# One decoder layer on one core: the first conv products on rows not yet normed, and conv taps ahead of their count from the heads' queries on

## The chip, the cores and the metric

The kernel runs on one core of a Trainium2 chip. The metric is device microseconds of one execution, start to end. TensorE is PE in the profile (its weight loads are PEld), VectorE is DVE, ScalarE is ACT, GpSimd is POOL, and SyncE, which issues most transfers, is SP.

## The reference

One layer of a decoder over 256 rows of 1024 channels, in fp32. Cut to what the change touches:

```python
n = RMSNorm(x)                       # x * rsqrt(mean(x*x) + eps) * g
a, gate, q, k, v, qi, ki, wi, gc, ga = split(n @ w_in)
u = a * sigmoid(gate)
u = causal_depthwise_conv(u, conv_w)           # 31 taps on each of 1024 channels
u = silu(LayerNorm(u)) @ w_conv_out
attn = top-k attention of q, k, v (keys chosen by qi, ki, wi), 8 heads
h = x + (gate_c * u + gate_a * attn @ w_attn_out) @ w_mix_out
h = h + CrossAttn(RMSNorm(h), RMSNorm(mem))    # xq, xk, xv, 4 heads
h = h + W2 relu(W1 RMSNorm(h))**2
return RMSNorm(h)
```

## The kernel before

Activations lie feature-major: a tile holds 128 channels on the partitions and the 256 rows along them. The weights are streamed from HBM in chunks of 1 MB, in a fixed order, by SP. Each half chunk is split into two parts for a matmul in fp32r: `hi` is a rounded copy (ScalarE, line 315) and `lo` is raw − hi (VectorE). The activations are split in the same way (n_p, o_p and so on). A product is then two matmuls for each tile of 128 channels, a wide one of hi against both parts and a narrow one of lo against the high part.

The first chunk, ("conv", 0), is an exception. It isn't split: PE multiplies it in native fp32, by n_f, the normed rows in full precision. It holds two tiles of products, the gate (`ps_conv00`) and the value (`ps_conv01`), eight products each. Behind it PE goes on with wide matmuls on n_p.

The norm at the start goes like this. PE transposes x_rm (the rows) to pt_n, ScalarE and VectorE scale it by the gain g_first to xg, the squares of the rows are summed meanwhile, and GpSimd takes the power −0.5 of them to rs_n (`power`). PE spreads rs_n over the partitions with two transposes against the identity, to ps_rsb_n (`spread`). VectorE multiplies xg by it to n_f, and n_f is split into n_p.

The 31 taps of the causal convolution run on VectorE, as acc += u · cw; some are made by ScalarE as products and added by a DMA of GpSimd, and some go by fours (ring and four). They are put into the order by `tick()`, which the code calls between its products. It keeps two sums of model time, pe.total and dve.total, in ns, and issues taps while

```python
while (...) and dve.total < pe.total - 1000:
    fill_one()
...
dve.total = max(dve.total, pe.total - 2000)
```

holds. The engines take their instructions in the order in which the program issues them, so this count decides only where the taps stand in VectorE's order, not when they run. When the taps of all channels are in, the last sums (usum, the sum over the eight tiles of acc) are added by VectorE, and `layer_norm` begins at the next tick: PE multiplies usum by a matrix of 1/1024 to ps_mub (the mean), VectorE subtracts it from acc, ScalarE squares, PE sums the squares to ps_vr, and ps_rsb spreads the reciprocal root of that. The chain is a generator, and takes a step at each tick. The product "co" reads its result.

Each head of the attention is a generator too: scores ps_s from q and k, a softmax on VectorE and ScalarE (att_t, att_p, sm), transposes ps_pt, the product ps_o with v, and its split to o_p (ScalarE the high part, VectorE the low). Products stand between these steps: q and k of the heads, then xk and xv of the cross attention (in kv), then ao.

PSUM banks come in three tags: mm (2), acc (4) and aux (2). `ps_turn` alternates between mm and acc.

Of the kernel before, what the change touches and what calls it, by code (L numbers as in the profile page):

```python
# [8 lines left out]
F32 = mybir.dt.float32  # L9
F32R = mybir.dt.float32r  # L10
BF16 = mybir.dt.bfloat16
AF = mybir.ActivationFunctionType
ALU = mybir.AluOpType
# [3 lines left out]
P = 128  # L17
D = 1024
S = 256
KT = D // P  # L20
# [101 lines left out]
def block_kernel(ctx, tc, x, xt, mem, memt, wst, wki, vecs, convw, gout, out):  # L122
    nc = tc.nc
    ctx.enter_context(tc.manual_schedule())
    pe = Counted(nc.tensor, pe_price)
    dve = Counted(nc.vector, dve_price)
    act = nc.scalar.activation
# [10 lines left out]
    def t8(name, dt=F32, shape=(P, KT, S)):  # L138
        return big.tile(list(shape), dt, tag="t8", bufs=12, name=name)
# [4 lines left out]
    def w2(name, dt=F32, shape=(P, 512)):  # L144
        return work.tile(list(shape), dt, tag="w2", bufs=8, name=name)
# [4 lines left out]
    def bank(tag, bufs, name):  # L150
        return psum.tile([P, 512], F32, tag=tag, bufs=bufs, name=name)

    def ps_mm(name):
        return bank("mm", 2, name)
# [4 lines left out]
    def ps_aux(name):  # L159
        return bank("aux", 2, name)  # L160

    mm_turn = [0]

    def ps_turn(name):

# [4 lines left out]
    prepared, whole, elsewhere = {}, {}, set()  # L170
# [5 lines left out]
    def fetch(c, raw, parts=1, only=None):  # L176

        key = STREAM[c]
        n = KT * NK if key[0] == "ki" else N_CHUNK
        src = wki if key[0] == "ki" else wst[INDEX[key]]  # L180
        for q in range(parts):
            if only in (None, q):
                ns = slice(q * n // parts, (q + 1) * n // parts)
                nc.sync.dma_start(raw[:, ns], src[:, ns])
        raw_of[c] = raw
        landed.update((key, q) for q in ((0, 1) if only is None else (only,)))

    def load(parts=1):
        if not order:
            return  # L190
        c = order.pop(0)
        key = STREAM[c]
        fetch(c, t8(f"raw{c}", F32, (P, N_CHUNK)) if c in early else raws.tile([P, N_CHUNK], F32, tag="raw", name=f"raw{c}"),
              2 if key in BY_HALVES else parts)
        if key[0] == "f2" and key[1] in ADDED:
            t = sums_of[c] = t8(f"sums{c}", F32, (P, 4, 512))
            blocks = wst[INDEX[key]].rearrange("p (j n) -> p j n", j=4)
            nc.gpsimd.dma_start(t[:, 0:2, :], blocks[:, 0:4:3, :])
            if key[1] == ALL_ADDED:
                nc.gpsimd.dma_start(t[:, 2:4, :], blocks[:, 0:4:2, :])  # L200
            nc.gpsimd.dma_start(t[:, 0:2, :], blocks[:, 1:2, :].to_broadcast([P, 2, 512]), accum_op=ALU.add)
            if key[1] == ALL_ADDED:
                nc.gpsimd.dma_start(t[:, 2:4, :], t[:, 1:2, :].to_broadcast([P, 2, 512]), accum_op=ALU.add)
                nc.gpsimd.dma_start(t[:, 3, :], blocks[:, 0, :], accum_op=ALU.add)
        if key in WHOLE:
            whole[key] = raw_of[c].rearrange("p (k n) -> p k n", k=2 * KT)
        elif c < FIRST:
            high_jobs.extend(jobs_of(c))
        elif c == FIRST:
            high_jobs.extend(last_jobs())  # L210
# [10 lines left out]
    def jobs_of(c):  # L221
        key = STREAM[c]
        if key[0] == "f2" and key[1] in SEVEN:
            return seven(key, c)
        n = KT * NK if key[0] == "ki" else N_CHUNK
        parts = 1 if key[0] == "ki" else 2
        ns = [slice(q * n // parts, (q + 1) * n // parts) for q in range(parts)]
        return [Stage((*key, q), lambda q=q: high(key, c, ns[q], q, q == parts - 1), slot=key != ("f2", 15),
                      needs=(key, q)) for q in range(parts)]
# [94 lines left out]
    def split_high():  # L324
        if high_jobs and high_jobs[0].here() and (not high_jobs[0].slot or nsplit[0] - nused[0] < HALVES - held[0]):
            job = high_jobs.pop(0)
            nsplit[0] += job.slot
            while job.steps:
                job.step()
            job.high()  # L330

    def split_low():
        if low_jobs:
            low_jobs.pop(0)()
        for job in high_jobs[:3]:
            if job.steps and job.here():
                job.step()
                break

    nsplit, nused, held = [0], [0], [1]  # L340
# [11 lines left out]
    chains, fours, fill, turn, done, ended = [], [], [], [0], [], []  # L352
# [16 lines left out]
    def split_ahead():  # L369
        split_low()  # L370
        split_high()

    def tick():
        for c in list(chains):
            if next(c, "end") == "end":
                chains.remove(c)
        while (len(fill) > 1 or (fill and (len(ended) > 5 or nused[0] < 5))) and dve.total < pe.total - 1000:
            fill_one()
        if fours and next(fours[0], "end") == "end":
            fours.clear()  # L380
        dve.total = max(dve.total, pe.total - 2000)
        add_some()

    def fill_one():

        some = [q for q in fill[:3] if q is not turn[0]] or fill
        q = some[0] if len(some[0]) < 10 and len(fill) > 3 else max(some, key=len)
        turn[0] = q
        q.pop(0)()
        if not q:  # L390
            fill.remove(q)
# [9 lines left out]
    def split(hi, lo, src):  # L401
        act(hi, src, AF.Copy)
        dve.tensor_tensor(out=lo, in0=src, in1=hi.bitcast(F32), op=ALU.subtract)
# [116 lines left out]
    half = cst.tile([P, 2], F32, name="half")  # L520
# [10 lines left out]
    ps = ps_aux("ps_warm")  # L531
# [22 lines left out]
    def spread(cols, name):  # L554

        ps = ps_aux(f"ps_{name}")
        for rb in range(2):
            pe.transpose(ps[:, rb * P : rb * P + P], cols[:, rb : rb + 1].to_broadcast([P, P]), ident)
        return ps[:, :S]
# [3 lines left out]
    n_f = t8("n_f")  # L563
    ss = small.tile([P, 2], F32, tag="ss", name="ss_n")
    ptn = [ps_acc(f"pt_n{c}") for c in range(4)]
    xg = t8("xg")
# [4 lines left out]
    for rb in range(2):  # L571
        for kt in range(KT):
# [5 lines left out]
                             in1=x_rm[:, 1, D // 2 :], scale=1.0 / D, scalar=EPS, op0=ALU.mult, op1=ALU.add,  # L578
                             accum_out=ss2[:, 1:2])
    dve.tensor_tensor(out=ss, in0=ss, in1=ss2, op=ALU.add)  # L580
    rs_n = power(ss, "n")
    rsb_n = spread(rs_n, "rsb_n")
    for kt in range(KT):
        src = ptn[kt // 2][:, (kt % 2) * S : (kt % 2) * S + S]
        if kt in (4, 6):
            dve.tensor_scalar(xg[:, kt, :], src, g_first[:, kt : kt + 1], None, ALU.mult)
        else:
            act(xg[:, kt, :], src, AF.Copy, scale=g_first[:, kt : kt + 1])
    for lo, hi in ((0, 1), (1, 2), (2, 4), (4, 6), (6, 8)):
        dve.tensor_tensor(out=n_f[:, lo:hi, :], in0=xg[:, lo:hi, :],  # L590
                          in1=rsb_n.unsqueeze(1).to_broadcast([P, hi - lo, S]), op=ALU.mult)
    for c in range(0, KT, 2):
        split(n2.high(c, 2), n2.low(c, 2), n_f[:, c : c + 2, :])
    split_high()
    split_low()
    split_high()
    pe.total = dve.total = 0.0

# [31 lines left out]
    u = t8("u")  # L630
# [74 lines left out]
    def conv_tile(i, half):  # L705
        key = ("conv", i)
        w = weights("conv", i, half, KT) if key not in WHOLE else None
        split_ahead()
        ps = (ps_turn if i > 0 else ps_mm)(f"ps_conv{i}{half}")
        if w:  # L710
            tile_b(ps, w, n2, wide=i > 0, back=back[0])
            back[0] = i > 0 and not back[0]
        else:
            for kt in range(KT):
                pe.matmul(ps[:, :S], whole[key][:, half * KT + kt, :], n_f[:, kt, :], start=kt == 0, stop=kt == KT - 1)
        return ps

    def conv_in(i):
        psg = conv_tile(i, 0)
        sg = w2(f"sg{i}", F32, (P, S))  # L720
        if i > 0:
            merge_now(sg, psg)
            act(sg, sg, AF.Sigmoid)
        else:
            act(sg, psg[:, :S], AF.Sigmoid)
        tick()
        psa = conv_tile(i, 1)
        if i > 0:
            merge_now(u[:, i, :], psa)
        dve.tensor_tensor(out=u[:, i, :], in0=u[:, i, :] if i > 0 else psa[:, :S], in1=sg, op=ALU.mult)  # L730
        tick()
        tap(i, 0)()
        queue = [tap(i, s) for s in range(1, TAPS) if s not in (*delays.get(i // 2, ()), *by_four.get(i // 4, ()))]
        queue.append(last_tap(i))
        if i // 2 not in delays:
            fill.append(queue)
        else:
            queues.setdefault(i // 2, []).append(queue)
            if i % 2:
                delay = iter(delays[i // 2])  # L740
                ready[i // 2] = lambda: add_tap(i // 2, next(delay))
        if ("conv", i) in WHOLE:
            load()

    for i in range(4):
# [10 lines left out]
    ps = ps_mm("ps_ki")  # L756
# [191 lines left out]
        headed.append(h)  # L948

    heads, headed = [], []  # L950

    def qk(name):
        return big.tile([P, 2, S], F32, tag="qk", bufs=4, name=name)
# [661 lines left out]
```

## Time and profile before

| | |
|---|---|
| time, median of 3 runs | 497.76 us (497.68 to 498.03) |
| profiled execution | 497.77 us |
| its span | 495.8 us |
| mean granted clock of TensorE | 0.997 |
| ScalarE busy | 377.6 us (76%) |
| GpSimd busy | 50.5 us (10%) |
| DMA, mean over the span | 223 GB/s, 110.36 MB |

The span runs from the first to the last instruction of the core, and the time of the execution holds 1.97 us around it. A timeline row of the profile has the start in us, the us from the first start to the last end of its group, the engine, the line, the operation, out<-in, the shape, how many instructions (x) and in brackets the idle time before them and what ended it. L87 is the line of the counting helper, so most instructions of PE and DVE carry it, and the names tell them apart.

### The profile page before, as it was taken

The page shows a single profiled execution, that of the slowest core. Times are in us where ns is not written, and L with a number is a line of the kernel's source. Part 1 is how long each engine was busy: PE and PEld are TensorE (multiplying, and loading weights), DVE is VectorE, ACT ScalarE, POOL GpSimd, SP SyncE. Part 2 cuts the span into 40 slices and gives each one's busy share as a digit, 9 for nine tenths or more (in the row PEclk, how much of TensorE's full clock was granted, in tenths as well). Part 3 has the DMA queues.
Part 4 walks back from the last instruction along what each step waited for, and adds up shares of the span by engine and source line. Part 5 has one row for each costly group of instructions (what it writes and reads, how often), then busy time and mean ns, then how long its engine had stood idle before and what let it go on. Part 6 is the DMA issues. An engine that isn't in the chain of part 4 may idle for free.

```text
span 495.8 us, 7787 instructions
## 1 busy us (share of the span) xinstructions
PE 486.5 (98%) x2832; PEld 428.0 (86%) x2832; DVE 460.1 (93%) x826; ACT 377.6 (76%) x677; POOL 50.5 (10%) x67
## 2 busy tenths in 40 slices
PE   7999999999999999999999999999999999999995
PEld 5888888888888889888889999988998888888884
DVE  5899999999999979989988987899999999999986
ACT  7578879998977787757946658687777878878852
POOL 2002211222011211000000000000010101121000
PEclk9999999999999999999999999999999999999998
DMA  8948676989987977354645552766979868999802
GB/s 315 380 190 262 191 190 212 277 234 248 283 247 215 243 166 209 134 171 169 254 171 177 205 203 97 278 193 144 255 263 296 247 238 258 283 318 341 260 3 85
DMA packets 33430, 110.36 MB, mean 223 GB/s; under 512 B 11104, under 2 KB 13408, under 8 KB 24432
## 3 DMA queue, kind: packets, MB, share of 16 engines
q1 hardware_dynamic: 24416, 93.03, 53.7%
q0 software_dynamic: 8688, 16.64, 17.6%
q8 instruction: 22, 0.36, 0.3%
q10 hardware_dynamic: 288, 0.20, 0.1%
q14 instruction: 16, 0.13, 0.1%
HBM read 99.29 MB, written 1.05 MB: 202 GB/s over the span
## 4 chain that ended last, share of the span: by engine, by line
PE 96%; DVE 1%; DMA 1%; ACT 1%; issue 0%; SPq 0%; DVEq 0%
PE ps_f L87 18%; PE ps_p L87 15%; PE ps_conv L87 9%; PE ps_co L87 5%; PE ps_ao L87 5%; PE ps_mix L87 5%; PE ps_k L87 5%; PE ps_ga L87 4%; PE ps_gc L87 4%; PE ps_q L87 4%; PE ps_v L87 4%; PE ps_xo L87 3%; PE ps_xq L87 2%; PE ps_xk L87 2%; PE ps_qi L87 2%; PE ps_xv L87 2%
## 5 line engine op out<-in xcount | busy, mean ns | idle before, releaser
L87 DVE TENSOR_TENSOR lo<-raw,hi 128x1024 fp32r<-128x1024 f32 x133 | 161.4, 1216 | 2.0 <-ACT hi L315 1.8
L315 ACT ACTIVATE hi<-raw 128x1024 fp32r<-128x1024 f32 x133 | 138.7, 1048 | 5.0 <-DMA raw<-in_wst_dram 5.0
L87 PE MATMUL ps_f<-ff_p,hi 128*128 128x512 f32 (+1 forms) x320 | 72.3, 347 | 0.0
L87 PEld LDWEIGHTS ps_f<-ff_p,hi 128*128 128x128 f32 x320 | 56.3, 189 | 7.9
L87 DVE SCALAR_TENSOR_TENSOR acc<-u,cw,acc 128x241 f32<-128x241 f32 (+25 forms) x142 | 58.9, 467 | 0.2
L87 PE MATMUL ps_f<-ff_p,lo 128*128 128x256 f32 x256 | 46.9, 283 | 0.0
L87 PEld LDWEIGHTS ps_f<-ff_p,lo 128*128 128x128 f32 x256 | 39.3, 191 | 1.8
L703 POOL DMA_DIRECT2D acc<-products x25 | 21.7, 879 | 123.3 <-ACT products L702 43.7
L87 PE MATMUL ps_conv<-n_p,hi 128*128 128x512 f32 x112 | 29.1, 396 | 0.0
L87 PEld LDWEIGHTS ps_conv<-n_p,hi 128*128 128x128 f32 x112 | 20.3, 188 | 4.5 <-issue 0.7
L293 ACT ACTIVATE inner<-sums 128x1024 fp32r<-128x1024 f32 x13 | 13.8, 1059 | 10.9 <-DVE sums L87 10.9
L702 ACT ACTIVATE products<-u,cw 128x243 f32<-128x243 f32 (+19 forms) x50 | 22.1, 492 | 0.0
L87 DVE TENSOR_TENSOR ft<-ft 128x128 f32<-128x128 f32 (+2 forms) x49 | 19.7, 401 | 1.1 <-ACT ft L1327 0.6
L671 ACT ACTIVATE ring<-u,cw 128x236 f32<-128x236 f32 (+10 forms) x44 | 20.2, 480 | 0.0
L87 PE MATMUL ps_p<-outer,fs 128*128 128x512 f32 x78 | 20.2, 394 | 0.0
L87 PE MATMUL ps_v<-hi,n_p 128*128 128x512 f32 x64 | 19.9, 389 | 0.0
L87 PE MATMUL ps_p<-inner,fs 128*128 128x512 f32 x78 | 19.8, 390 | 0.0
L87 PE MATMUL ps_co<-u_p,hi 128*128 128x512 f32 (+1 forms) x80 | 19.3, 350 | 0.0
L87 PE MATMUL ps_mix<-mix_p,hi 128*128 128x512 f32 (+1 forms) x80 | 19.2, 349 | 0.0
L87 PE MATMUL ps_k<-n_p,hi 128*128 128x512 f32 x64 | 17.4, 404 | 0.0
L87 PE MATMUL ps_q<-n_p,hi 128*128 128x512 f32 x64 | 17.3, 402 | 0.0
L87 PEld LDWEIGHTS ps_p<-inner,fs 128*128 128x128 f32 x78 | 14.6, 188 | 3.0
(443 smaller groups left out, 1212.4 us busy)
## 6 DMA issues: line engine op xcount, KB each, us to landing
raw<-in_wst_dram SPq DMA_DIRECT2D x67, 1024.0 KB, 5.9
raw<-in_wst_dram SPq DMA_DIRECT2D x28, 512.0 KB, 5.8
sums<-in_wst_dram POOLq DMA_DIRECT2D x15, 512.0 KB, 7.6
acc<-products POOLq DMA_DIRECT2D x25, 256.0 KB, 6.1
x_rm<-in_x_dram SPq DMA_DIRECT2D x2, 512.0 KB, 4.0
mem_rm<-in_mem_dram SPq DMA_DIRECT2D x1, 1024.0 KB, 8.7
mem_t<-in_memt_dram SPq DMA_DIRECT2D x1, 1024.0 KB, 10.7
h_t<-in_xt_dram SPq DMA_DIRECT2D x1, 1024.0 KB, 7.7
```

The source lines that it names most:

```text
L87: return fn(*args, **kwargs)
L293: act(hi, src, AF.Copy)
L315: act(hi, raw[:, ns], AF.Copy)
L671: act(dst[:, t, :], u[:, 4 * g + t, : S - s], AF.Copy, scale=cw[:, 4 * g + t, TAPS - 1 - s : TAPS - s])
L702: act(prod[:, a, s:], u[:, t, : S - s], AF.Copy, scale=cw[:, t, TAPS - 1 - s : TAPS - s])
L703: nc.gpsimd.dma_start(acc[:, ts, :], prod, accum_op=ALU.add)
```

## The change

It has three parts.

1. The native products read xg, the rows with the gain but not yet divided by their root mean square. Two products of `ps_conv00` stand ahead of the transposes of rs_n in PE's order, the six others and those of `ps_conv01` behind them. The missing factor, one per row, is brought in later: ScalarE copies ps_rsb_n to SBUF (`rsb`) behind the second n_p, VectorE multiplies ps_conv00 by it ahead of the sigmoid, and multiplies the sigmoid's result by it ahead of the product with ps_conv01. One `split_low` moves from the start to behind `conv_in(0)`.
2. `mm_turn` begins at 1, so every bank that `ps_turn` gives changes its tag.
3. The count of the taps gets its 1000 from `spare[0]`, and that is −1500 from the heads' queries on: taps are issued until dve.total is 1500 ahead of pe.total, not until it is 1000 behind.

```diff
-    mm_turn = [0]
+    mm_turn = [1]
...
+    spare = [1000]
     def tick():
...
-        while (len(fill) > 1 or (fill and (len(ended) > 5 or nused[0] < 5))) and dve.total < pe.total - 1000:
+        while (len(fill) > 1 or (fill and (len(ended) > 5 or nused[0] < 5))) and dve.total < pe.total - spare[0]:
             fill_one()
...
-    rsb_n = spread(rs_n, "rsb_n")
...
+    first = whole["conv", 0]
+    ps_first = ps_mm("ps_conv00")
+    def first_products(kts):
+        for kt in kts:
+            pe.matmul(ps_first[:, :S], first[:, kt, :], xg[:, kt, :], start=kt == 0, stop=kt == KT - 1)
+    first_products(range(2))
+    rsb_n = spread(rs_n, "rsb_n")
+    rsb = w2("rsb", F32, (P, S))
...
         split(n2.high(c, 2), n2.low(c, 2), n_f[:, c : c + 2, :])
+        if c == 2:
+            act(rsb, rsb_n, AF.Copy)
     split_high()
-    split_low()
     split_high()
...
+        if (i, half) == (0, 0):
+            first_products(range(2, KT))
+            return ps_first
...
-                pe.matmul(ps[:, :S], whole[key][:, half * KT + kt, :], n_f[:, kt, :], start=kt == 0, stop=kt == KT - 1)
+                pe.matmul(ps[:, :S], whole[key][:, half * KT + kt, :], xg[:, kt, :], start=kt == 0, stop=kt == KT - 1)
...
         else:
-            act(sg, psg[:, :S], AF.Sigmoid)
+            dve.tensor_tensor(out=sg, in0=psg[:, :S], in1=rsb, op=ALU.mult)
+        act(sg, sg, AF.Sigmoid)
         tick()
         psa = conv_tile(i, 1)
...
+        else:
+            dve.tensor_tensor(out=sg, in0=sg, in1=rsb, op=ALU.mult)
...
         if ("conv", i) in WHOLE:
+            split_low()
             load()
...
     heads, headed = [], []
+    spare[0] = -1500
```

PE's order at the start, before. pt_n are the transposes of x, ps_conv_203 and ps_conv_218 the two tiles of native products, ps_conv_237 the first of the wide ones:

```order
L87 MATMUL pt_n_131<-ident,x_rm 128x128 x2
L87 MATMUL ps_rsb_n<-ident,rs_n 128x128 x2
L87 MATMUL ps_conv_203<-n_f,raw_89 128x256 x8
L87 MATMUL ps_conv_218<-n_f,raw_89 128x256 x8
L87 MATMUL ps_conv_237<-n_p_124,hi_0_183 128x512 x4
```

And after:

```order
L87 MATMUL pt_n_131<-ident,x_rm 128x128 x2
L87 MATMUL ps_conv_167<-xg,raw_89 128x256 x2
L87 MATMUL ps_rsb_n<-ident,rs_n 128x128 x2
L87 MATMUL ps_conv_167<-xg,raw_89 128x256 x6
L87 MATMUL ps_conv_220<-xg,raw_89 128x256 x8
L87 MATMUL ps_conv_241<-n_p_124,hi_0_188 128x512 x4
```

Two products have moved ahead of the transposes of rs_n, and all sixteen read xg.

VectorE's order at the first query, before; acc<-u,cw,acc is one tap, lo_0_1612 and q_1606 belong to the half chunk and the result of the first q:

```order
L87 TENSOR_TENSOR four_924<-four_924,ring_925 128x4x231
L87 TENSOR_TENSOR lo_1_1582<-raw_1458,hi_1_1581 128x1024
L87 SCALAR_TENSOR_TENSOR acc<-u,cw,acc 128x234
L87 TENSOR_TENSOR lo_0_1612<-raw_1510,hi_0_1611 128x1024
L87 TENSOR_TENSOR q_1606<-ps_q_1614,q_1606 128x256
```

And after:

```order
L87 TENSOR_TENSOR four_923<-four_923,ring_924 128x4x231
L87 TENSOR_TENSOR lo_1_1583<-raw_1459,hi_1_1582 128x1024
L87 SCALAR_TENSOR_TENSOR acc<-u,cw,acc 128x234
L87 SCALAR_TENSOR_TENSOR acc<-u,cw,acc 128x244
L87 SCALAR_TENSOR_TENSOR acc<-u,cw,acc 128x233
L87 SCALAR_TENSOR_TENSOR acc<-u,cw,acc 128x243
L87 SCALAR_TENSOR_TENSOR acc<-u,cw,acc 128x232
L87 SCALAR_TENSOR_TENSOR acc<-u,cw,acc 128x242
L87 SCALAR_TENSOR_TENSOR acc<-u,cw,acc 128x231
L87 SCALAR_TENSOR_TENSOR acc<-u,cw,acc 128x241
L87 TENSOR_TENSOR lo_0_1613<-raw_1511,hi_0_1612 128x1024
L87 TENSOR_TENSOR q_1607<-ps_q_1615,q_1607 128x256
```

Eight taps stand there where one stood; ahead of these rows three taps are gone, and behind them VectorE stays four taps further on than before until the taps end.

VectorE's order at the last taps and the sums of the layer norm, before; o_p_1605 is the low part of head 5, kv the result of xk:

```order
L87 TENSOR_TENSOR o_p_1605<-ps_o_2365,o_p_1605 128x256
L87 RECIPROCAL sm_2281<-sm_2281 128x2
L87 TENSOR_TENSOR kv<-ps_xk_2301,kv 128x256
L87 SCALAR_TENSOR_TENSOR acc<-u,cw,acc 128x239
L87 SCALAR_TENSOR_TENSOR acc<-u,cw,acc 128x238 x2
L87 TENSOR_TENSOR acc<-acc,four_924 128x4x237
L87 TENSOR_TENSOR usum<-usum,acc 128x256
L87 TENSOR_TENSOR lo_1_2346<-raw_2127,hi_1_2345 128x1024
L87 RECIPROCAL sm_2334<-sm_2334 128x2
L87 TENSOR_TENSOR kv<-ps_xk_2348,kv 128x256
L87 TENSOR_TENSOR lo_0_2388<-raw_2215,hi_0_2387 128x1024
L87 SCALAR_TENSOR_TENSOR acc<-u,cw,acc 128x238
```

The three other sums into usum follow these rows. And after:

```order
L87 TENSOR_TENSOR o_p_1606<-ps_o_2372,o_p_1606 128x256
L87 RECIPROCAL sm_2289<-sm_2289 128x2
L87 TENSOR_TENSOR kv<-ps_xk_2309,kv 128x256
L87 SCALAR_TENSOR_TENSOR acc<-u,cw,acc 128x238
L87 TENSOR_TENSOR acc<-acc,four_923 128x4x237
L87 TENSOR_TENSOR usum<-usum,acc 128x256 x4
L87 TENSOR_TENSOR lo_1_2353<-raw_2135,hi_1_2352 128x1024
```

The sums now stand in one piece behind head 5's o_p and kv, one tap and one add of four tiles.

PE's order at the mean of the layer norm, before; ps_xv is the first product of xv, which takes four quarters of its weights (hi_0, hi_1 of two chunks), and ps_o and ps_pt belong to the last two heads:

```order
L87 MATMUL ps_xv_2383<-lo_0_2299,mem_p_191 128x512
L87 MATMUL ps_xv_2383<-hi_0_2298,mem_p_191 128x512
L87 MATMUL ps_o_2452<-ptr_2426,v_rm 128x128 x3
L87 MATMUL ps_pt_2458<-ident,att_p_2372 128x128 x3
L87 MATMUL ps_mub<-usum,onesd 128x256
L87 MATMUL ps_xv_2382<-hi_1_2345,mem_p_191 128x512
```

And after:

```order
L87 MATMUL ps_xv_2391<-lo_0_2225,mem_p_194 128x512
L87 MATMUL ps_xv_2391<-hi_0_2224,mem_p_194 128x512
L87 MATMUL ps_mub<-usum,onesd 128x256
L87 MATMUL ps_xv_2390<-hi_1_2260,mem_p_194 128x512
L87 MATMUL ps_xv_2390<-lo_1_2261,mem_p_194 128x512
```

ps_mub stood between the third and the fourth quarter of xv and now stands between the first and the second. With it ps_vr moves from behind the third of ao's eight tiles to behind the first, and ps_rsb from behind the fourth to behind the second.

More of the change, by code (lines that the diff above doesn't have):

```diff
@@ L720, in conv_in @@
         sg = w2(f"sg{i}", F32, (P, S))
-        if i > 0:
+        if i:
             merge_now(sg, psg)
-            act(sg, sg, AF.Sigmoid)
         else:
-            act(sg, psg[:, :S], AF.Sigmoid)
+            dve.tensor_tensor(out=sg, in0=psg[:, :S], in1=rsb, op=ALU.mult)
+        act(sg, sg, AF.Sigmoid)
         tick()
         psa = conv_tile(i, 1)
-        if i > 0:
+        if i:
             merge_now(u[:, i, :], psa)
-        dve.tensor_tensor(out=u[:, i, :], in0=u[:, i, :] if i > 0 else psa[:, :S], in1=sg, op=ALU.mult)
+        else:
+            dve.tensor_tensor(out=sg, in0=sg, in1=rsb, op=ALU.mult)
+        dve.tensor_tensor(out=u[:, i, :], in0=u[:, i, :] if i else psa[:, :S], in1=sg, op=ALU.mult)
         tick()
```

## The prediction

> **What bounds the kernel now.** I read the page's first and fourth parts, then the waits of TensorE (PE) and of its weight loads (PEld), then the timeline at the three places that the order moves. From the page:
>
> ```profile
> span 495.8 us, 7787 instructions
> PE 486.5 (98%) x2832; PEld 428.0 (86%) x2832; DVE 460.1 (93%) x826; ACT 377.6 (76%) x677; POOL 50.5 (10%) x67
> PE 96%; DVE 1%; DMA 1%; ACT 1%; issue 0%; SPq 0%; DVEq 0%
> ```
>
> PE is busy for 98% of the span and is 96% of the chain that ended last. VectorE (DVE), at 93%, is second. So the time falls only where PE waits now, and it grows wherever PE comes to wait. The view of waits, PE's three rows and the one PEld row that the bank order touches (us in total, times, longest):
>
> ```profile
> PE ps_warm L533 <- DVE zero_r L517: 1.9, 1, 1.9
> PE ps_rsb_n L87 <- POOL rs_n L538: 0.9, 1, 0.9
> PE ps_conv L87 <- DVE n_f L87: 0.6, 1, 0.6
> PEld ps_conv L87 <- ACT sg L725: 0.2, 1, 0.2
> ```
>
> These are all of PE's waits, and all lie before 16 us. Part one of the change can win at most 0.9 + 0.6 = 1.5 us of wait, and the transposes' 0.43 us stay. At the heads and the layer norm PE waits for nothing: there the change can't win, only lose.
>
> **Part one: the native products on rows not yet normed.** The timeline of the start, and the landing of the first half chunk (KB, us from issue to landing):
>
> ```profile
> 1.64 2.43 SPq L184 DMA_DIRECT2D raw<-in_wst_dram  x5
> ...
> 4.43 2.31 PE L87 MATMUL pt_n<-ident,x_rm 128*128 128x128 f32 x16
> ...
> 6.26 2.27 ACT L588 ACTIVATE xg<-pt_n,g_first 128x256 f32<-128x256 f32 x6
> ...
> 6.88 0.72 POOL L538 TENSOR_TENSOR rs_n<-ss_n,half 128x2 f32<-128x2 f32 x1 [3.84 <-DVE ss_n L87]
> ...
> 7.65 0.43 PE L87 MATMUL ps_rsb_n<-ident,rs_n 128*128 128x128 f32 x2 [0.90 <-POOL rs_n L538]
> 8.19 2.55 DVE L87 TENSOR_TENSOR n_f<-xg,ps_rsb_n 128x256 f32<-128x256 f32 x5 [0.64 <-ACT xg L588]
> ...
> 8.67 7.24 PE L87 MATMUL ps_conv<-n_f,raw 128*128 128x256 f32 x32 [0.58 <-DVE n_f L87]
> ...
> 10.66 2.49 DVE L87 TENSOR_TENSOR n_p<-n_f,n_p 128x512 fp32r<-128x512 f32 x4
> ...
> 13.06 3.57 DVE L87 TENSOR_TENSOR lo<-raw,hi 128x1024 fp32r<-128x1024 f32 x3
> ...
> 15.70 2.11 PE L87 MATMUL ps_conv<-n_p,hi 128*128 128x512 f32 x8
> ...
> 17.65 1.11 PE L87 MATMUL ps_conv<-n_p,lo 128*128 128x256 f32 x8
> ```
> ```profile
> raw<-in_wst_dram SPq DMA_DIRECT2D x1, 512.0 KB, 6.3
> ```
>
> PE has done the transposes of x at 4.43 + 2.31 = 6.74. The first xg is there at about 6.26 + 0.45 = 6.71: six start within 2.27, the last runs some 0.45, so one starts each (2.27 − 0.45)/5 = 0.36. But the products also read the weights: the first half chunk is issued at 1.64 and lands after 6.3, at 7.94. So the first product starts at about 7.98, not at 6.75. It hardly passes the transposes of rs_n, which could go at 7.65: the two products (16 products in 32 passes of 7.24 − 0.22 over the 31 starts between, 0.22 a pass, hence two products of two passes 0.9, with the change of weights 0.96) run to 8.95, the transposes take 0.35 to 9.30, and the 14 others 14 × 0.431 = 6.03. The wide matmuls start at 15.33 instead of 15.70: **−0.35**. If weights did not gate, all 16 products would follow 6.75 and the gain would be near the whole 1.5; if the second half, issued just behind, landed late, it is zero. Neither is excluded; I take the landing, since its row is measured for that very transfer.
>
> What it costs elsewhere: rs_n's transposes end 9.30 instead of 8.08, so n_f and the n_p pairs are 1.2 later and ScalarE's copy of rsb, the size of an xg, adds some 0.4 to its row of n_p highs. The last n_p low was done at 10.66 + 2.49 = 13.15, now at about 14.45; the wide matmuls need the first at 15.33, the last pairs about 1 us later. The first lo was done at 13.06 + 1.22 = 14.28, now 15.6, and PE reads it at 17.65 − 0.35 = 17.3. Two more multiplies of 128x256 on VectorE, 0.43 each, stand behind ps_conv00 and ahead of u; nothing of PE's waits for u before taps and layer norm. All this is hidden by 0.8 us or more: 0 (0 to +0.8, if it all ends late).
>
> **Part two: bank parity.** ps_conv10 goes to a bank that isn't read by the sigmoid at 15.3; the 0.2 us wait of PEld ends. PE's row shows no wait of its own beside it, so I count none of it, 0 (−0.2 to 0). The other banks of this turn come back to PE 1.2 us or more after their last reader (from the bank tags and the timeline); 0.
>
> **Part three: the taps from the queries on.** At the first head's tick VectorE gets 8 taps instead of 1, and 3 fewer ahead of it. The timeline there:
>
> ```profile
> 140.25 0.48 ACT L671 ACTIVATE ring<-u,cw 128x230 f32<-128x230 f32 x1
> ...
> 141.06 1.12 DVE L87 TENSOR_TENSOR four<-four,ring 128x924 f32<-128x924 f32 x1
> ...
> 145.07 1.22 DVE L87 SCALAR_TENSOR_TENSOR acc<-u,cw,acc 128x241 f32<-128x241 f32 x3
> ...
> 146.20 1.23 DVE L87 TENSOR_TENSOR lo<-raw,hi 128x1024 fp32r<-128x1024 f32 x1
> ...
> 150.93 0.43 DVE L87 TENSOR_TENSOR k<-ps_k,k 128x256 f32<-128x256 f32 x1
> ...
> 153.47 0.82 PE L87 MATMUL ps_s<-k,q 128*128 128x128 f32 x4
> ```
>
> A tap costs (146.20 − 145.07)/3 = 0.377 of VectorE. Seven more are 2.64. The three that are gone ahead of it save VectorE 1.13, but the `four` add behind them needs ScalarE's ring, done 140.25 + 0.48 = 140.73, so it starts 0.33 earlier at most. VectorE is thus 2.31 late. PE's first scores read k, which VectorE finished at 150.93 + 0.43 = 151.36, 2.11 ahead of 153.47. PE waits 2.31 − 2.11 = 0.2, with the semaphore **+0.25** (0 if VectorE catches up by a queued read; 0.6 if the three saved taps bring nothing). Everything else that PE takes from VectorE there has more room (the lo parts 5 us or more).
>
> Then the layer norm. Its mean product ps_mub moves two quarters of xv up in PE's order, and the adds into usum follow kv directly. The timeline before:
>
> ```profile
> 203.45 0.42 DVE L87 TENSOR_TENSOR o_p<-ps_o,o_p 128x256 fp32r<-128x256 f32 x1 [0.82 <-ACT o_p L402]
> ...
> 205.96 0.83 PE L87 MATMUL ps_o<-ptr,v_rm 128*128 128x128 f32 x6
> ...
> 206.82 0.39 ACT L402 ACTIVATE o_p<-ps_o 128x256 fp32r<-128x256 f32 x1 [0.88 <-PE ps_o L87]
> ...
> 207.51 0.42 DVE L87 TENSOR_TENSOR o_p<-ps_o,o_p 128x256 fp32r<-128x256 f32 x1
> ...
> 207.92 0.41 DVE L87 TENSOR_TENSOR kv<-ps_xk,kv 128x256 f32<-128x256 f32 x1
> ...
> 208.24 1.22 DVE L87 SCALAR_TENSOR_TENSOR acc<-u,cw,acc 128x239 f32<-128x239 f32 x3
> ...
> 209.17 0.62 PE L87 MATMUL ps_xv<-hi,mem_p 128*128 128x512 f32 x2
> ...
> 209.49 1.15 DVE L87 TENSOR_TENSOR acc<-acc,four 128x948 f32<-128x948 f32 x1
> ...
> 210.67 0.42 DVE L87 TENSOR_TENSOR usum<-usum,acc 128x256 f32<-128x256 f32 x1
> ...
> 214.06 1.34 DVE L87 TENSOR_TENSOR usum<-usum,acc 128x256 f32<-128x256 f32 x3
> ...
> 216.19 0.60 PE L87 MATMUL ps_mub<-usum,onesd 128*128 128x256 f32 x2
> ...
> 228.53 0.51 PE L87 MATMUL ps_vr<-onesd,vs 128*128 128x2 f32 x4
> ```
>
> Before, usum was done at 214.06 + 1.34 = 215.40, 0.79 ahead of ps_mub. The place to which ps_mub moves is ahead of the second of the two matmuls in the row of 209.17, where PE comes at 209.40. When can usum be done? The o_p of head 5 stands ahead of it on VectorE. It needs ScalarE's part, which ends 206.82 + 0.39 = 207.21, and that part needs ps_o of PE: however far VectorE is ahead, o_p can't start before 207.27. From there, with the spacings of the rows: kv 0.41 later (207.92 − 207.51), 207.68; one tap 0.32 behind it, 208.00; the `four` add 0.50 behind a last tap (209.49 − 208.99, the third start of the row at 208.24), 208.50; the first usum add 1.18 behind that, 209.68; three more at 0.46 (1.34 less the 0.42 of one, over two), 211.04; its end 211.46. PE waits from 209.40 to 211.46, **+2.1**. At the short end VectorE waits less for ScalarE and its adds run at 0.42 a start, +1.7; at the long end it comes to o_p as late as before, and a lo goes between, +3.0. I take the middle, which is what the rows give without either. PE has no slack after it with which to win this back, since it is the bound to the end.
>
> The sums of the layer norm that follow move with ps_mub: ps_vr and ps_rsb are two tiles of ao earlier, 13.6 us of PE's work behind ps_mub (the durations of what now stands between) where there were 228.53 − 216.19 = 12.3, so VectorE and ScalarE have 1.3 us more for it; 0. SP's order of transfers is the same, and POOL's differs by one exchange of two neighbours; 0. VectorE as a whole gets two multiplies, 0.86 us against 35 us of idle; 0.
>
> **The sum.** 497.77 (this execution; its span 495.8 and 1.97 around it; the median of the runs is 497.76, so the same) − 0.35 + 0.25 + 2.1 = **499.8 us**, a span of 497.8. The likeliest's own range, with the bounds of its three terms: 498.8 to 500.8.
>
> **The rivals.**
>
> *ps_mub does not wait* (the other side). The burst leaves VectorE ahead, and if usum were done by 209.4 nothing but the start would count: 497.77 − 0.35 = 497.4. For it: VectorE has four taps more behind it from the queries on, 4 × 0.377 = 1.5. Against it: that lead is lost wherever VectorE stands for PE, and it does so here:
>
> ```profile
> 177.61 0.42 DVE L87 TENSOR_TENSOR o_p<-ps_o,o_p 128x256 fp32r<-128x256 f32 x1 [2.46 <-ACT o_p L402]
> ```
>
> It idled 2.46 before this o_p and 0.82 before that of 203.45. It decides from the point at which o_p could start at 205.2, and PE's ps_o isn't issued by then. Chance 0.10, the same within 0.2%.
>
> *The weights do not gate the start.* Products from 6.75 on, −1.5 instead of −0.35, with ps_mub's wait as forecast: 498.6, the same (0.05); without that wait too: 497.77 − 1.5 = 496.3, faster (0.04). For it: the two waits of 0.9 and 0.6 name rs_n and n_f, not raw. Against it: ps_conv came at 8.67, after raw's 7.94, so a wait for raw could not show before.
>
> *The clock falls in the new gap.* A wait of 2 us is PE's longest after 10 us. At the end of the kernel PE has no matmul from 489.95 on, and the windows (us, PE busy, granted clock, DMA share, GB/s) show when the clock follows:
>
> ```profile
> 489.95:493.00 3.05, 0.00 (x0) 1.00 0.05 17
> 493.00:494.00 1.00, 0.00 (x0) 0.56 1.02 367
> ```
>
> It is full for some 3.1 us without a matmul and halved after that. If a gap of 2.1 to 3.0 were enough, and the clock stayed low for about as long as it took to fall, 3.1 us would do half their work, +1.5: 501.3. Against it: the gap is shorter than 3.1. Chance 0.05. The Trainium skill ("TensorE: Matmul & The Clock Gate", "HAM oscillation") says that an idle gap of more than about 3.4 us of TensorE returns it to half its clock, by a window that runs freely; by that rule this gap is too short, and only at the long end would it come near. The end of this trace agrees with it, at 3.1.
>
> *The change doesn't do what it says.* The taps would be no further ahead at the layer norm, because VectorE's place there is set by head 5's o_p and not by the taps. That is in the forecast already; if the burst changed nothing else, ps_s0 would not wait either: 499.5, inside the likeliest's range.
>
> **How the numbers follow.** ps_mub waits about 2 us, 0.76; no wait at ps_mub, 0.10; the start gains all, 0.05 with ps_mub's wait and 0.04 without; the clock falls, 0.05. The measurement can tell about 0.2%, 1.0 us, so slower begins at 498.8, where the likeliest's range begins. Slower: 0.76 + 0.05 = 0.81; same: 0.10 + 0.05 = 0.15; faster: 0.04. The range for 8 in 10 leaves out the faster case, the clock and the outer ends of the likeliest, and so reaches down to the case without a wait: 497.4 to 501.0.
>
> **What would show it.** In the waits of the changed kernel: PE ps_mub <- DVE usum, about 2.1; PE ps_s <- DVE k, about 0.25; a first ps_conv at 8.0 that waits for the DMA of raw, with ps_rsb_n behind it at about 9; wide matmuls from 15.3. The granted clock stays at 1.00 around 210. Wrong it would be if ps_mub shows no wait, if the first product starts before 7.5, or if the time behind 216 grows by more than PE has lost by then.

## The result, and the profile after

The changed kernel is slower: 501.74 us (median of 11 runs, 500.20 to 503.35) against 497.96 (11 runs) of the kernel before, a ratio of 1.006 with an interval of 1.0032 to 1.0087. Most kernels here, the one before too, have a few executions that take several us longer than their others (one is shown with the last experiment), so medians say more below than such a ratio.

The profiled execution took 501.52 us, its span 3.6 more than before. The first lines of its page and PE's waits (us in total, times, longest):

```profile
span 499.4 us, 7793 instructions
PE 489.3 (98%) x2832; PEld 430.3 (86%) x2832; DVE 460.7 (92%) x828; ACT 378.4 (76%) x678; POOL 51.4 (10%) x67
PE 74%; DVE 20%; issue 3%; ACT 1%; POOL 1%; DVEq 0%; POOLq 0%
```
```profile
PE ps_mub L87 <- DVE usum L87: 1.9, 1, 1.9
PE ps_warm L535 <- DVE zero_r L519: 1.9, 1, 1.9
PE ps_s L87 <- DVE k L87: 0.3, 1, 0.3
```

The waits for rs_n and n_f are gone and two new ones have come, both for VectorE. The chain of the page shows the same: it now runs back through VectorE (20%) from the wait at ps_mub on, since that wait joins PE's end to the taps.

The start, in the timeline of the changed kernel:

```profile
4.42 3.40 PE L87 MATMUL pt_n<-ident,x_rm 128*128 128x128 f32 x16
...
7.85 1.10 PE L87 MATMUL ps_conv<-xg,raw 128*128 128x256 f32 x4
8.79 0.38 PE L87 MATMUL ps_rsb_n<-ident,rs_n 128*128 128x128 f32 x2
9.01 6.21 PE L87 MATMUL ps_conv<-xg,raw 128*128 128x256 f32 x28
...
14.87 2.20 PE L87 MATMUL ps_conv<-n_p,hi 128*128 128x512 f32 x8
```

The wide matmuls start at 14.87 where they started at 15.70: 0.83 won. Then the layer norm:

```profile
207.13 0.42 DVE L87 TENSOR_TENSOR o_p<-ps_o,o_p 128x256 fp32r<-128x256 f32 x1
...
207.55 0.40 DVE L87 TENSOR_TENSOR kv<-ps_xk,kv 128x256 f32<-128x256 f32 x1
...
207.87 0.46 DVE L87 SCALAR_TENSOR_TENSOR acc<-u,cw,acc 128x238 f32<-128x238 f32 x1
...
208.36 1.15 DVE L87 TENSOR_TENSOR acc<-acc,four 128x948 f32<-128x948 f32 x1
...
209.06 0.39 PE L87 MATMUL ps_xv<-hi,mem_p 128*128 128x512 f32 x1
...
209.54 1.80 DVE L87 TENSOR_TENSOR usum<-usum,acc 128x256 f32<-128x256 f32 x4
...
211.39 0.70 PE L87 MATMUL ps_mub<-usum,onesd 128*128 128x256 f32 x2 [1.94 <-DVE usum L87]
```

VectorE goes without a pause from head 5's o_p to the end of usum at 211.34, and PE stands from 209.45 to 211.39. What follows is in the windows (us, PE busy and matmuls, granted clock, DMA share, GB/s):

```profile
209.50:211.30 1.80, 0.00 (x0) 1.00 0.00 0
211.40:212.20 0.80, 0.80 (x4) 1.00 0.00 0
212.20:215.60 3.40, 3.40 (x10) 0.51 0.53 178
215.60:217.00 1.40, 1.40 (x9) 0.98 0.75 316
```

PE is busy again at 211.4, and 0.8 us later its clock is halved, for 3.4 us: 10 matmuls where an execution with a full clock makes 18 (in the last experiment).

Lined up matmul by matmul against the profile before, PE is 0.83 early at the wide matmuls, 0.70 at 41 us, 0.10 behind ps_s, then 2.35 late right behind ps_mub and 4.15 late behind the half clock. Some of that comes back where ps_mub, ps_vr and ps_rsb used to stand: at 240 us it is 3.60 late, and it ends 3.62 late. Another execution of the same kernel, with a full clock behind ps_mub (the one of 500.10, in the last experiment), is 0.10 early behind ps_s too, and 2.01 late at 240 us. So: start −0.83, small losses to 41 us +0.13, ps_s +0.60, ps_mub +2.11, half clock +1.59, the rest +0.02: +3.62.

### The profile page after: what moved, and what is told of

Its sections match the earlier page's. It is cut to its first block, busy times and chain, and to the rows that moved or that the text cites. A ratio compares the mean times of both kernels' runs of the same rounds, so it can differ in the third digit from the quotient of the medians.

```text
span 499.4 us, 7793 instructions
## 1 busy us (share of the span) xinstructions
PE 489.3 (98%) x2832; PEld 430.3 (86%) x2832; DVE 460.7 (92%) x828; ACT 378.4 (76%) x678; POOL 51.4 (10%) x67
## 4 chain that ended last, share of the span: by engine, by line
PE 74%; DVE 20%; issue 3%; ACT 1%; POOL 1%; DVEq 0%; POOLq 0%
PE ps_f L87 18%; PE ps_p L87 15%; DVE lo L87 7%; DVE acc L87 5%; PE ps_conv L87 5%; PE ps_co L87 5%; PE ps_mix L87 5%; PE ps_ao L87 4%; PE ps_k L87 3%; PE ps_xo L87 3%; PE ps_q L87 3%; PE ps_xq L87 2%; PE ps_qi L87 2%; PE ps_xv L87 2%; DVE picked L87 2%
## 5 line engine op out<-in xcount | busy, mean ns | idle before, releaser
L87 DVE SCALAR_TENSOR_TENSOR acc<-u,cw,acc 128x241 f32<-128x241 f32 (+22 forms) x142 | 58.3, 464 | 0.1
```

The lines of the kernel that those rows point to most:

```text
L87: return fn(*args, **kwargs)
```

## The experiments

Theory A: the start is a gain; the loss is VectorE's lateness at ps_s and ps_mub and the half clock that the second wait causes. Theory B, its rival, is named in each expectation.

**Parts one and two alone.**

```diff
-    spare[0] = -1500
```

> The changed kernel without its line spare[0] = -1500: parts one and two alone. Theory A (the loss is ps_mub's wait for usum and the half clock that follows it, the start is a gain): PE's wide matmuls still start 0.8 us earlier than in the kernel before, PE has no wait from 20 us on, and the time is the time before less 0.7 to 0.8, 497.0 to 497.2. Rival B (the start costs something that the changed kernel's trace hides, such as later taps): 497.8 or more.

Measured: 498.98 (median of 12, 498.79 to 507.85), ratio 1.0055 (1.002 to 1.009). Slower than before by about 1 us: theory A's number was missed, rival B was right. Its waits and ps_mub:

```profile
PE ps_warm L535 <- DVE zero_r L519: 1.9, 1, 1.9
PE ps_co L87 <- DVE u_p L87: 0.6, 2, 0.3
PE ps_co L87 <- ACT u_p L916: 0.3, 1, 0.3
```
```profile
218.96 0.60 PE L87 MATMUL ps_mub<-usum,onesd 128*128 128x256 f32 x2
```

PE is 0.76 early at the wide matmuls, and 0.64 to 0.75 for most of the way to "co". There it waits for u_p and ends 0.95 late, a loss of 1.7. The reason lies in the count. Part one puts two products of PE before the reset of the count (2 × 427 ns by the price in the code), adds two multiplies to VectorE behind it (2 × 337 ns) and one lo that had stood before it (1137 ns). By the count VectorE is then busier than it was, so fewer taps are issued: in the order, three fewer ahead of the first query. The taps end later, ps_mub stands at 218.96 instead of 216.19, and the layer norm's result comes too late for "co". So the first part has a cost 230 us behind it, in the order alone. The run with −200 in the count, below, takes this cost away; the change's −1500 goes further than that.

**Part three alone.**

```diff
     def tick():
-        while (...) and dve.total < pe.total - 1000:
+        while (...) and dve.total < pe.total - spare[0]:
...
     heads, headed = [], []
+    spare[0] = -1500
```

> The kernel before with the count's line alone: part three alone. Theory A: ps_mub waits about 2 us for usum, ps_s 0.3 to 0.5 for k, and the clock halves for about 3.4 us behind ps_mub in some of the executions: 500.4 without that and 502.1 with it, so a spread of 1.7 where the kernel before has 0.3. Rival B (the wait needs the start's change too, since it brings VectorE out of step): 498.3 or less, no wait at ps_mub over 1 us.

Measured: 499.78 (6 runs, 499.51 to 501.12), ratio 1.0038 (1.0024 to 1.0052). The wait is there without the start's change, shorter, and this profile keeps a full clock behind it (it is of the execution of 501.12, which has another wait of 1.3 us, of ps_f at 454 us):

```profile
PE ps_mub L87 <- DVE usum L87: 1.4, 1, 1.4
```
```profile
212.00:216.00 4.00, 4.00 (x21) 1.00 0.57 207
```

Rival B is out; theory A's 2 us was 1.4, and no second group of times near 502 came in these six.

**ps_mub back at its old place, the taps as changed.**

```diff
     def layer_norm():
         u2.append(parts_t8("u_p"))
+        yield
+        yield
```

> The changed kernel with two yields at the start of the layer norm's chain, which puts ps_mub, ps_vr and ps_rsb back to the places that they had before; the taps stay as the change has them. Theory A: no wait at ps_mub, the clock full throughout, 497.2 to 497.6 (the start's -0.8, the taps' +0.3 to +0.5 at ps_s). Rival B (the burst of taps itself costs the time, ps_mub only shows it): 499.5 or more, with another wait in ps_mub's place.

Measured: 497.90 (12 runs, lowest 497.50), ratio 1.0009 (0.9984 to 1.0033): as the kernel before. One new wait is left:

```profile
PE ps_s L87 <- DVE k L87: 0.5, 1, 0.5
```

So moving ps_mub and what follows from it by two ticks is worth 3.8 us of the median (501.74 − 497.90). The time was 0.3 above theory A's range: PE was 0.55 early at 41 us, lost 0.63 at ps_s and some 0.3 more in small steps up to 188 us. The burst ahead of k thus takes all that the start gave.

**PE kept busy in the wait.**

```diff
-        mub = ps_mm("ps_mub")[:, :S]
+        mub = ps_mm("ps_mub")
+        for _ in range(2):
+            nc.tensor.matmul(mub, onesd, v_rm[:, 0, :512], start=True, stop=True)
+        mub = mub[:, :S]
```

> The changed kernel with two fp32 matmuls of 128x512 more (onesd by v_rm, results thrown away), ahead of ps_mub in its bank: some 1.7 us of work for PE inside the gap in which it waits for usum, so that the gap without a matmul is under 0.4 us. Theory A (the gap itself lowers the clock): the wait ends at the same time, the clock stays full behind it, and the time is 499.8 to 500.4 with the spread gone. Rival B (the lower clock is a state of the execution that has nothing to do with the gap): as the changed kernel, 500.2 to 503.4 with the same spread.

Measured: 500.10 (6 runs, 499.90 to 500.73), ratio 1.0043 (1.0031 to 1.0054).

```profile
209.61 1.88 PE L888 MATMUL ps_mub<-v_rm,onesd 128*128 128x512 f32 x4
211.71 0.70 PE L87 MATMUL ps_mub<-usum,onesd 128*128 128x256 f32 x2 [0.22 <-DVE usum L87]
```

ps_mub comes 0.3 later than in the changed kernel, with useless work before it, and the time is 1.6 lower in the median, as theory A has it: of six executions none went above 500.73, where 7 of the changed kernel's 11 took 501.5 or more. It is the gap that lowers the clock; why not each time, the last experiment shows.

**A longer gap.** Three operations more on VectorE ahead of ps_mub.

```diff
         u2.append(parts_t8("u_p"))
+        for _ in range(3):
+            nc.vector.tensor_tensor(out=usum, in0=usum, in1=usum, op=ALU.max)
```

> The changed kernel with three more operations of VectorE (usum = max(usum, usum), which changes nothing) ahead of ps_mub: PE's gap grows by about 1.3 us, to about 3.3. Theory A (a gap lowers the clock by a window that runs freely, and the longer it is the surer): the clock halves behind ps_mub in all executions or nearly all, for 3.4 us or more; 501.5 + 1.3 = 502.8 and not below 502. Rival B (the clock has nothing to do with the gap): the changed kernel's spread moved by 1.3, 501.5 to 504.6.

Measured: 505.30 (4 runs, 505.20 to 505.71), ratio 1.015 (1.0137 to 1.0163). The gap grew more than meant, since a lo and a kv stand between usum and the added operations on VectorE. The windows and the wait:

```profile
PE ps_mub L87 <- DVE usum L887: 4.7, 1, 4.7
```
```profile
210.10:212.20 2.10, 0.00 (x0) 1.00 0.00 0
212.30:214.70 2.40, 0.00 (x0) 0.52 0.21 41
214.80:219.10 4.30, 4.30 (x10) 0.50 0.54 217
```

The clock is halved from 212.3 to 219.1, 6.8 us or two times 3.4, the first part of it while PE still waits, and all four executions lie within 0.5 us. So the drop came in all four, as far as times tell. The time expected, 502.8, was for a gap of 3.3 and one low stretch of 3.4; of the 2.5 above it the longer gap makes 1.4, a longer wait at ps_s (0.89 against 0.34) some 0.55, and 4.5 us of work at half clock in place of 3.4 some 0.5.

**A shorter wait: one tick.**

```diff
         u2.append(parts_t8("u_p"))
+        yield
```

> The changed kernel with one yield at the start of the layer norm's chain: ps_mub stands one quarter of xv (1.4 us) further back. Theory A: its wait for usum falls from 1.9 to about 0.6, the clock stays full, and the time is 498.2 to 498.6, with the spread of the kernel before. Rival B (a wait of any length lowers the clock): 499.9 or more in some executions.

Measured: 499.39 (5 runs, 499.15 to 500.94), ratio 1.0036 (1.0024 to 1.0048). ps_mub doesn't wait at all, but something else does:

```profile
PE ps_ao L87 <- DVE o_p L87: 1.2, 1, 1.2
```
```profile
219.44 0.63 ACT L895 ACTIVATE sq_vr<-acc 128x512 f32<-128x512 f32 x1 [0.57 <-DVE acc L87]
...
222.06 0.38 ACT L404 ACTIVATE o_p<-ps_o 128x256 fp32r<-128x256 f32 x1
...
222.48 0.42 DVE L87 TENSOR_TENSOR o_p<-ps_o,o_p 128x256 fp32r<-128x256 f32 x1 [1.33 <-ACT o_p L404]
```

The layer norm's steps come one tick later and now stand, on ScalarE and VectorE, ahead of the last head's o_p. In the kernel before, o_p was done at 221.61, just in time for the last of the eight high parts of the first ao tile; here PE waits 1.16 for it, to 222.96. The profile keeps a full clock. Theory A was right on ps_mub and wrong on the time, by this wait.

**The count set so that the heads get the taps they had.**

```diff
-    spare[0] = -1500
+    spare[0] = -200
```

> The changed kernel with -200 in place of -1500 in its count. By the order of instructions this gives VectorE the same number of taps ahead of every q, k and o_p of the heads as the kernel before, and ps_mub, ps_vr and ps_rsb stand where they stood before; parts one and two are kept. Theory A (the start is a real gain, which the changed kernel loses at ps_s and ps_mub, and the kernel without the count's line loses at ps_co): no wait from 20 us on, the start's -0.7 to -0.8 arrives at the end: 497.0 to 497.3. Rival B (what the start wins is taken back by something else on the way, as it would be by transfers): 497.8 or more.

Measured: 496.87 (median of 11), against 497.82 of the kernel before beside it (17 runs, none under 497.68). Ten of the eleven lie between 496.81 and 497.37; the eleventh, 503.78, makes the ratio 0.9994 (0.9971 to 1.0018). PE's waits and its first products:

```profile
PE ps_warm L535 <- DVE zero_r L519: 1.9, 1, 1.9
PE ps_conv L87 <- DMA raw<-in_wst_dram: 1.0, 1, 1.0
```
```profile
7.79 1.10 PE L87 MATMUL ps_conv<-xg,raw 128*128 128x256 f32 x4 [0.96 <-DMA raw<-in_wst_dram]
8.72 0.38 PE L87 MATMUL ps_rsb_n<-ident,rs_n 128*128 128x128 f32 x2
...
14.80 1.50 PE L87 MATMUL ps_conv<-n_p,hi 128*128 128x512 f32 x5
```

The heads get the number of taps that they had, by the trace within one. There is no wait after the start, PE is 0.90 early at the wide matmuls, 0.76 at 41 us and 0.77 at the end. This is the version that beats both: the start's gain arrives when the taps are paced as before. It also shows what gates the start. PE was free at 6.8 and waited 0.96 for the weights, which landed at 7.65.

**The same with the first chunk in four parts.**

```diff
-    for parts in (2, 2, 1):
+    for parts in (4, 2, 1):
         load(parts)
```

> The changed kernel with -200 in its count (as in the run before of that value) and the first chunk fetched in four parts of 256 KB instead of two of 512 KB. Theory A (where the transposes of x run at full clock, the first products wait for the landing of the weights, 7.7 us): the first part lands near 7.0, and the wide matmuls start up to 0.6 us earlier where the transposes end at 6.8, and no earlier where they end at 7.8: 496.3 to 496.9. Rival B (the landing isn't what they wait for, or the two more issues on SP delay the chunks behind): 496.8 to 497.6.

Measured: 496.99 (median of 12, 496.93 to 498.14), ratio 0.9961 (0.9931 to 0.9992). No gain over the two parts, though a second time faster than the kernel before.

```profile
7.60 1.10 PE L87 MATMUL ps_conv<-xg,raw 128*128 128x256 f32 x4 [0.25 <-ACT xg L589]
```

The row names xg, but the first xg was done at about 7.2; the first part of the weights landed at 7.46, not at 7.0: with half the bytes it came only 0.2 earlier than the half chunk of the run before (7.65). PE's last matmul ended 0.21 earlier than in that run (488.95 against 489.16), while the span is 0.1 longer; what took it back stands behind PE's last matmul.

**The same with the old bank parity.**

```diff
-    mm_turn = [1]
+    mm_turn = [0]
```

> The changed kernel with -200 in its count and mm_turn at 0, as in the kernel before: what part two, the bank parity, is worth. Theory A (it takes away a wait of PEld of 0.2 us for a bank, which now ends later, since the sigmoid's operand waits for a multiply): 0 to 0.3 us over the same kernel with mm_turn at 1, 496.9 to 497.2. Rival B (a bank of the other parity stalls PE somewhere later): above 497.4.

Measured: 497.82 (median of 12, 497.69 to 499.27), 0.95 above the same kernel with the new parity, which ran on another chip (the lowest time of the kernel before was 497.68 on both). Theory A's 0 to 0.3 was too little; PE does stall, though for the same bank and not later as rival B had it, and it costs the whole gain.

```profile
PE ps_conv L87 <- DVE sg L87: 0.8, 1, 0.8
```
```profile
15.47 0.41 DVE L87 TENSOR_TENSOR sg<-ps_conv,rsb 128x256 f32<-128x256 f32 x1
...
16.03 1.17 PE L87 MATMUL ps_conv<-n_p,hi 128*128 128x512 f32 x4 [0.80 <-DVE sg L87]
```

With the old parity the first wide product takes the bank that ps_conv00 is in. That bank is read by the new multiply, which stands behind a lo on VectorE and ends at 15.88. PE starts at 16.03 instead of 14.80. The 0.2 us wait of PEld in the profile before became 0.8 of PE.

**The changed kernel again.** Six executions beside the version with −200, then two single ones.

> The changed kernel once more, unchanged, beside the others on the same chip. Theory A: its times fall into groups, near 500.2 where the clock stays full behind ps_mub and near 501.8 where it halves for 3.4 us. Rival B (the groups are of the chip, not of the kernel): the kernel before, which runs beside it, shows such groups as well.

> The changed kernel once more, for its profile. Theory A (the window that decides on the clock runs freely, so the same wait at ps_mub can pass at full clock): if the time is near 500.2, the granted clock stays at 1.00 behind ps_mub; if it is near 501.7, it is 0.50 for 3.4 us. Rival B: a time near 500.2 with the clock lowered, or one near 501.7 without.

> As the look before: near 500.2 with a full clock behind ps_mub, or near 501.7 with 3.4 us of half clock; any other pairing speaks for rival B.

The six runs of the first: 500.03, 500.51, 501.54, 501.66, 501.77, 503.00, median 501.60, ratio 1.0071 (1.0056 to 1.0085); the kernel before, beside it, has 16 of 17 within 497.68 to 498.46. The profiled one, 501.66, has the half clock behind ps_mub. The first of the two single executions, 500.10:

```profile
PE ps_mub L87 <- DVE usum L87: 1.9, 1, 1.9
```
```profile
209.50:211.30 1.80, 0.00 (x0) 1.00 0.00 0
...
212.20:215.60 3.40, 3.40 (x18) 1.00 0.61 186
```

The same wait at the same place, and the clock stays full: 18 matmuls in those 3.4 us. Span for span this is 1.4 less than in the first profile (498.0 against 499.4). So the gap of 1.94 us lowers the clock in some executions and not in others, and that makes the two groups. The other single execution, 505.04, has a full clock behind ps_mub too and another loss, earlier:

```profile
188.90 0.86 ACT L685 ACTIVATE ring<-u,cw 128x226 f32<-128x226 f32 x2 [7.78 <-DMA four<-ring]
...
191.13 1.65 PE L87 MATMUL ps_o<-ptr,v_rm 128*128 128x128 f32 x6 [3.47 <-ACT ptr L958]
```

ScalarE stood 7.78 us for an addition that GpSimd makes by DMA, with ptr behind it, and PE stood 3.47. That transfer took 9.5 us, no longer than in the execution of 500.10 (9.6), but it was issued 6.2 us later (179.38 against 173.19); what delayed it was not followed up. PE's wait of 3.47 us halved the clock, and the later one at ps_mub, of 1.94 us (214.60 to 216.54), did not. The wait and the half clock make most of the 4.9 between 505.04 and 500.10. The windows:

```profile
190.00:191.00 1.00, 0.00 (x0) 0.94 0.00 0
191.00:192.00 1.00, 0.87 (x4) 0.50 0.80 105
...
215.00:216.00 1.00, 0.00 (x0) 1.00 0.00 0
216.00:217.00 1.00, 0.46 (x3) 1.00 0.00 0
217.00:218.00 1.00, 1.00 (x6) 1.00 0.00 0
```

This was neither theory, so a time alone doesn't tell which cause it has; that the runs of 502.5 to 503.4 have such a cause was not seen in a profile and stays open.

The traces do show what decides between the two groups. In each of them the clock changes only at whole multiples of 3.413 us from the point at which it first rises: in the profile of 501.52 it rises at 7.44 and falls at 212.24, 60 × 3.413 later; in that of 505.04 it rises at 6.56 and falls at 190.88, 54 × 3.413 later. So time is cut into windows of 3.413 us, and what counts is how much of a gap lies in one window:

| execution | window (us) | PE idle in it (us) | clock behind it |
|---|---|---|---|
| changed, 501.52 | 208.83 to 212.24 | 1.94, the whole gap | half |
| changed, 501.66 | 209.14 to 212.56 | 1.94, the whole gap | half |
| changed, 500.10 | 206.59 to 210.00 | 0.55 | full |
| the same | 210.00 to 213.42 | 1.39 | full |
| changed, 505.04 | 187.46 to 190.88 | 3.22 | half |
| the same | 214.77 to 218.18 | 1.77 | full |
| part three alone, 501.12 | 208.16 to 211.57 | 1.44 | full |
| a longer gap, 505.28 | 208.98 to 212.39 | 2.35 | half |
| the same | 212.39 to 215.80 | 2.37 | half |

In all fourteen profiles here, their ends included, no window with less than 1.8 us of idle was followed by a lower clock, and every one with 1.9 or more was. The gap at ps_mub is long enough where one window holds it whole, and was too short where a boundary split it. With 1.94 us in windows of 3.413 that is, as an estimate from these two numbers, 43% of the positions ((3.413 − 1.94) / 3.413), or a little more if somewhat less than 1.94 is enough. Of the changed kernel's 14 executions near either time, 7 lie at 500.0 to 500.5 and 7 at 501.5 to 501.9.

## Why the prediction was right and where it was not

The direction and the place were right: slower, by a wait of PE at ps_mub for usum. That the executions with a full clock come within 0.3 of the forecast is partly luck: up to 41 us PE won 0.70 where 0.35 was set, and at ps_s it lost 0.60 where 0.25 was set, so two errors of 0.35 cancel. By its steps:

- *The start, −0.35.* It was −0.83, and the step that failed is the sum of the durations, each a little long (its own 15.33 against 15.70 is −0.37). The gate was as forecast: the first products came at 7.79 (with −200), by the landing, and at 7.85 in the changed kernel, where the transposes of x ended later than the landing. Both are earlier than the 7.98 of the forecast, since the weights landed 0.2 earlier than in the profile before. Then the transposes of rs_n took 0.22 where 0.35 was set, and the fourteen products 5.86 where 6.03 was set; for the 0.431 of one product no working is given, and measured it was 0.42.
- *Cover at the start, 0.* n_p and lo came in time: no wait there in any profile with the new parity.
- *Part two, 0 (−0.2 to 0).* Wrong as a step. It costed the wait that was there, not the one that part one would make of it: the multiply reads the bank later than the sigmoid did. Without part two the gain is lost (497.82 against 496.87).
- *ps_s, +0.25.* Right in kind, a wait of 0.34, and more than twice the size in PE's lateness, 0.60. k was done at 153.22, 1.86 later than before where 2.31 was forecast; but PE came there 0.70 earlier by the start, and the forecast didn't add that gain to the wait.
- *ps_mub, +2.1.* The wait was 1.94, and PE's lateness grew by 2.11 in the end. The chain was as the rows said: o_p at 207.13 (207.27), usum done at 211.34 (211.46).
- *The clock, a rival with 0.05.* This is the term that was missing, and the sign "the granted clock stays at 1.00 around 210" did not come. It was set aside since PE had been idle for 3.1 us at the end before its clock fell. But that was the distance from PE's last matmul to the next window boundary (489.93 to 493.12), not the length that a gap must have: in the run with ps_mub at its old place the clock falls 2.2 us after the last matmul (490.39 to 492.61). A gap of 1.94 was enough in two of the four profiles of the changed kernel, and cost 1.59, near the 1.5 of the rival. The median of 501.74 lies above the forecast's 499.8 and its upper end of 501.0; the ratio of 1.006 on 497.76 would be 500.7. With a full clock the changed kernel takes 500.1, 0.3 from the forecast.
- *The rule beside it.* "TensorE: Matmul & The Clock Gate" of the Trainium skill, in "HAM oscillation", has it that a gap must pass about 3.4 us. Here the measurement differs: 1.94 us could do it, where it lay in one window. The length of the low stretch, 3.41 us, and that the window runs freely agree with the page: the low stretch is one window long, and the boundaries lie at another place in each execution (the clock first rises anywhere from 5.02 to 8.25 us).
- *The rival without a wait* did not come in the changed kernel. It came as the version with −200: 496.87, where it was given 497.4.
- *The ranges.* The likeliest's 498.8 to 500.8 is not what the bounds of its terms give: −0.35, 0 to 0.6 and 1.7 to 3.0 on 497.77 make 499.1 to 501.0.

## What to carry to other kernels

A count of model time that paces one engine's filler carries every change at its start through the whole order: where work is moved across the point at which the count is reset, compare the orders at the far end, not at the change. Move the matmul that needs a late sum no further than the sum's chain allows, which is bounded by the last thing that PE itself must do first. And an idle gap of the bound engine costs more than its length: here a wait of 1.94 us cost 2.1, and 3.7 where the clock fell, and filling the gap with useless matmuls took the surcharge away. Whether the clock falls hangs on where the gap lies in a window, so one profile of such a kernel shows one of two times.

## What was not expected of the hardware

That less than 2 us without a matmul can halve the clock, that the same gap passes in other executions, and that the clock can fall 0.85 us after PE is busy again (211.39 and 212.24): all three follow from windows of 3.413 us.

The start shows the same windows. The transposes of x follow each other at 0.21 us and, from one point on, at 0.11. That point is where the trace's first record of a full clock begins: 5.02 in the profile before, 5.39 with −200, 7.44 in the changed kernel's first profile, where only the last transpose comes behind it. Ahead of that record the trace holds none, and the view of windows prints 1.00 there. The window that ends at the first rise holds 3.08 us or more of PE's work in all fourteen profiles, and the window before it 2.89 or less. In the changed kernel's first profile that window runs from 4.03 to 7.44 and is filled by transposes from 4.42 on, so transposes count as work in it. Whether the transposes end at 6.8 or at 7.8, and whether the gap at ps_mub costs 1.59 more, thus hang on the same thing, the place of the windows in that execution.
